# Prefix log-sum-exp along the sequence: a fourth load up front and an early store of part of the first tile on ScalarE's DMA ring

## Chip, cores and metric

One core of a Trainium2 chip, the other cores idle. The metric is the device time of one execution in microseconds (us); the profile's span, from the first to the last instruction, is some 1.8 us shorter. The runs of one kernel agree within 0.2%.

Three words are used throughout. A *ring* is the queue of transfers that one engine issues (SyncE's and ScalarE's here). A *run* is a stretch of consecutive bytes; the trace records each run as one packet. A transfer *lands* when the trace shows it complete, which releases those that wait for it.

## The reference

```python
# x: (4, 4096, 4128) float32
out[:, 0, :] = x[:, 0, :]
for t in range(1, S):
    mx = np.maximum(out[:, t - 1, :], x[:, t, :])
    out[:, t, :] = mx + np.log(np.exp(out[:, t - 1, :] - mx) + np.exp(x[:, t, :] - mx))
```

So out[t] is the logarithm of the running sum of exp(x), per column. The arrays are 270.5 MB each; every byte is read once and written once.

## The kernel before

A tile (a `Step`) holds 128 partitions x `r` consecutive rows x 4128 columns in float32; `r` is 3, or 2 for the first tile of the first sequence and the last tile of the others. It is worked on in place, in four chunks of 1024 columns (the last with 32 more, the tail). For each chunk ScalarE writes exp(x) as 16-bit numbers into the front half of the chunk's own columns, TensorE sums them into PSUM with triangular weights, and ScalarE writes the logarithm, row by row, over the same columns in 32 bits. When all chunks are done SyncE stores the tile.

```python
def load(self):
    full = xpool.tile([P, R, D], FP32, name="xt")      # 4 buffers
    self.xt = full[:, :self.r, :]
    self.half = self.xt.bitcast(FP16)                  # a 16-bit view of the same bytes
    nc.sync.dma_start(out=self.xt, in_=self.dram(x))

def store(self):
    nc.sync.dma_start(out=self.dram(out), in_=self.xt)

# Chunk
def exp(self):
    c0, w = self.c * CH, self.w
    nc.scalar.activation(
        self.t.half[:, :, 2 * c0:2 * c0 + w], self.t.xt[:, :, c0:c0 + w], ACT.Exp,
    )

def stage(self, j):
    t, c, pt = self.t, self.c, self.pt
    nc.scalar.activation(t.xt[:, j, c * CH:(c + 1) * CH], pt, ACT.Ln)
    # ... the next row's sum, or the carry to the next tile

# the order of issue
ahead = bufs - 1
for s in steps[:ahead]:
    s.load()
# ...
for g in range(len(chunks) + R - 1):
    for d in range(R - 1, -1, -1):
        if 0 <= g - d < len(chunks) and d < chunks[g - d].t.r:
            k = chunks[g - d]
            k.stage(d)
            if k.c == last and d + 1 == k.t.r:
                k.t.store()
                if stored + ahead < len(steps):
                    steps[stored + ahead].load()
                stored += 1
    if g + 2 < len(chunks):
        chunks[g + 2].exp()
    if g + 1 < len(chunks):
        chunks[g + 1].head()
```

Waits are not in the source: the tile framework works them out from which instruction reads and writes which part of a tile.

The softmax here doesn't subtract the row's maximum and nothing guards it: scores larger than these inputs give would overflow.

## Time and profile before

| | before |
|---|---|
| time, median of 4 runs | 1262.91 us |
| bytes over DMA | 541.07 MB |
| DMA engines (16), share of the span on SyncE's queue | 99.4% |
| rate at full DMA share | 432 to 436 GB/s |
| ScalarE busy | 75% |

The lines behind this table are in the prediction. One is the start of ScalarE's work, in the timeline (start, length in us, engine, line, operation, out<-in, count, and in brackets the idle time before it and what ended it). Before:

```profile
19.79 2.00 ACT L162 ACTIVATE xt<-pt 128x1024 f32<-128x1024 f32 x2
21.69 1.96 ACT L128 ACTIVATE xt<-xt 128x2112 f16<-128x2112 f32 x1
23.68 1.95 ACT L162 ACTIVATE xt<-pt 128x1024 f32<-128x1024 f32 x2
27.68 2.76 ACT L128 ACTIVATE xt<-xt 128x3072 f16<-128x3072 f32 x1 [2.06 <-DMA xt<-in_x_dram]
```

The first line is two logarithms, the second of chunk 0 and the first of chunk 1; the next is the exponential of chunk 3 (2 x 1056 = 2112 columns).

### The profile page before, as it was taken

What the parts mean: (1) busy time and instruction counts of PE and PEld (TensorE: products, weight loads), DVE (VectorE), ACT (ScalarE), POOL (GpSimd) and SP (SyncE); (2) the same over time, 40 slices, a digit from 0 to 9 for tenths busy, and PEclk for the clock granted to TensorE, in tenths of its full rate; (3) what the DMA queues carried; (4) which work ended last, traced back from release to release, by engine and by line L of the source; (5) the groups of instructions that cost most, each with busy time, mean ns of one, the idle gap of its engine ahead of it and who ended that gap; (6) DMA issues with size and microseconds to landing.
All of it is one profiled execution on the core that took longest, in us unless ns stands there. A gap on an engine that the chain in (4) does not pass through costs nothing.

```text
span 1261.0 us, 6165 instructions
## 1 busy us (share of the span) xinstructions
PE 688.7 (55%) x2268; PEld 237.0 (19%) x2268; DVE 451.4 (36%) x445; ACT 947.3 (75%) x733; POOL 2.2 (0%) x13
## 2 busy tenths in 40 slices
PE   3665554555555555655346555555634755664552
PEld 1222111111121111211112211111211211221120
DVE  2443333333333333334424333333442433333344
ACT  5997777777777777778569777777966977777794
POOL 0000000000000000000000000000000000000000
PEclk9887777777677777777768777787777777778786
DMA  9999999999999999999999999999999999999998
GB/s 411 410 439 431 432 427 434 438 430 432 433 437 431 432 432 436 432 427 436 431 433 436 437 429 431 436 436 432 430 434 435 432 431 432 434 435 431 433 422 347
DMA packets 12702, 541.46 MB, mean 429 GB/s; under 512 B 1408, under 2 KB 1408, under 8 KB 1408
## 3 DMA queue, kind: packets, MB, share of 16 engines
q1 hardware_dynamic: 12672, 541.07, 99.4%
q8 instruction: 18, 0.29, 0.1%
q14 instruction: 12, 0.10, 0.0%
HBM read 270.53 MB, written 270.53 MB: 429 GB/s over the span
## 4 chain that ended last, share of the span: by engine, by line
DMA 69%; ACT 21%; PE 5%; issue 2%; DVE 1%; SPq 0%; ACTq 0%
DMA xt<-in_x_dram 67%; ACT xt L128 11%; ACT xt L162 10%; PE pt L88 5%; DMA out_dram<-xt 2%; ACT xt L167 0%; SPq L116 0%; DVE carry L92 0%; DVE carry L93 0%; ACTq L231 0%; SPq L113 0%; ACTq L128 0%; PE qt L88 0%
## 5 line engine op out<-in xcount | busy, mean ns | idle before, releaser
L128 ACT ACTIVATE xt<-xt 128x3072 f16<-128x3072 f32 (+3 forms) x176 | 478.5, 2719 | 247.9 <-DMA xt<-in_x_dram 247.8
L88 PE MATMUL pt<-xt,ident 128*128 128x512 f16 x672 | 251.3, 470 | 530.7 <-ACT xt L162 530.4
L162 ACT ACTIVATE xt<-pt 128x1024 f32<-128x1024 f32 x512 | 487.6, 1030 | 2.5 <-PE pt L88 0.7
L92 DVE CAST carry<-pt 32x1024 f16<-32x1024 f32 x176 | 216.4, 1230 | 761.0 <-ACT xt L162 760.7
L88 PE MATMUL pt<-xt,excl 128*128 128x512 f16 x672 | 247.0, 504 | 0.0
L93 DVE TENSOR_TENSOR carry<-pt,carry 32x1024 f16<-32x1024 f32 x176 | 215.9, 1227 | 6.1
L88 PEld LDWEIGHTS <-ident 128*128 128x128 f16 x672 | 70.1, 104 | 677.7 <-issue 654.0
L88 PE MATMUL pt<-xt,incl 128*128 128x512 f16 x352 | 152.0, 526 | 23.6 <-ACT xt L128 15.0
L88 PEld LDWEIGHTS <-excl 128*128 128x128 f16 x756 | 92.5, 124 | 141.0 <-issue 108.1
L88 PE MATMUL pt<-carry,pick 128*128 128x512 f16 x320 | 109.8, 429 | 0.0
L88 PEld LDWEIGHTS <-incl 128*128 128x128 f16 x480 | 45.2, 111 | 129.7 <-DVE carry L93 95.2
L88 PEld LDWEIGHTS <-pick 128*128 128x128 f16 x360 | 40.6, 113 | 57.0 <-issue 34.3
L167 ACT ACTIVATE xt<-qt 128x96 f32<-128x96 f32 (+1 forms) x44 | 10.9, 249 | 45.7 <-PE pt L88 45.7
L92 DVE CAST carry_t<-qt 32x32 f16<-32x32 f32 x44 | 8.7, 197 | 25.5 <-ACT xt L167 25.4
L88 PE MATMUL qt<-xt,incl 128*128 128x64 f16 (+2 forms) x128 | 12.3, 196 | 0.0
L88 PE MATMUL qt<-xt,excl 128*128 128x64 f16 (+1 forms) x84 | 10.6, 187 | 0.0
L93 DVE TENSOR_TENSOR carry_t<-qt,carry_t 32x32 f16<-32x32 f32 x44 | 8.5, 193 | 1.5
L88 PE MATMUL qt<-carry_t,pick 128*128 128x96 f16 (+1 forms) x40 | 8.2, 204 | 0.0
L83 DVE MEMSET carry<- 128x512 uint32 x4 | 1.9, 485 | 1.1 <-PEq L220 1.0
L70 ACT ACT_TABLE_LOAD x1 | 1.3, 1283 | 0.8 <-PEq L220 0.8
L35 POOL TENSOR_SCALAR_AFFINE_SELECT pick<-pick 128x128 f16<-128x128 f16 x2 | 0.6, 294 | 0.1
L25 POOL TENSOR_SCALAR_AFFINE_SELECT incl<-incl 128x128 f16<-128x128 f16 x1 | 0.3, 294 | 0.0
(11 smaller groups left out, 1.9 us busy)
## 6 DMA issues: line engine op xcount, KB each, us to landing
xt<-in_x_dram SPq DMA_DIRECT2D x40, 6192.0 KB, 42.2
out_dram<-xt SPq DMA_DIRECT2D x40, 6192.0 KB, 28.1
xt<-in_x_dram SPq DMA_DIRECT2D x4, 4128.0 KB, 37.3
out_dram<-xt SPq DMA_DIRECT2D x4, 4128.0 KB, 23.0
```

What stands on the lines that cost most here:

```text
L25: nc.gpsimd.affine_select(out=t, in_=t, pattern=[[1, P]], compare_op=mybir.AluOpType.is_ge, fill=0.0, base=base, channel_multiplier=-1,)
L35: nc.gpsimd.affine_select(out=t, in_=t, pattern=[[step, P]], compare_op=mybir.AluOpType.not_equal, fill=1.0, base=base, channel_multiplier=1,)
L70: nc.scalar.preload_act_table_set("natural_log_exp_and_others")
L83: nc.vector.memset(t, 0.0)
L88: nc.tensor.matmul(pt, lhsT=w, rhs=rhs, start=start, stop=stop, skip_group_check=True)
L92: nc.vector.tensor_copy(cr[HI:HI + 32, :], pt[HI:HI + 32])
L93: nc.vector.tensor_tensor(out=cr[LO:LO + 32, :], in0=pt[HI:HI + 32], in1=cr[HI:HI + 32, :], op=mybir.AluOpType.subtract,)
L128: nc.scalar.activation(self.t.half[:, :, 2 * c0:2 * c0 + w], self.t.xt[:, :, c0:c0 + w], ACT.Exp,)
L162: nc.scalar.activation(t.xt[:, j, c * CH:(c + 1) * CH], pt, ACT.Ln)
L167: nc.scalar.activation(t.xt[:, :, t0:D], self.qt, ACT.Ln)
```

## The change

The intent, as far as the code shows it: keep loads in the queue past the first store, and take whatever a first store costs early, on another ring, while loads go on. Four loads are issued up front instead of three, and as soon as chunk 0 of the first tile is finished, its 1024 columns (2 rows of 4096 bytes in each partition, 1.05 MB) are stored by ScalarE's ring. The tile's later store on SyncE's ring leaves these columns out.

```diff
         def store(self):
-            nc.sync.dma_start(out=self.dram(out), in_=self.xt)
+            a = self.apart
+            nc.sync.dma_start(out=self.dram(out)[:, :, a:], in_=self.xt[:, :, a:])
+
+        def store_apart(self):
+
+            a = self.apart = CH
+            nc.scalar.dma_start(out=self.dram(out)[:, :, :a], in_=self.xt[:, :, :a])
...
-    for s in steps[:ahead]:
+    for s in steps[:bufs]:
         s.load()
...
                 k.stage(d)
+                if k is chunks[0] and d + 1 == k.t.r:
+                    k.t.store_apart()
                 if k.c == last and d + 1 == k.t.r:
                     k.t.store()
-                    if stored + ahead < len(steps):
+                    if bufs <= stored + ahead < len(steps):
                         steps[stored + ahead].load()
```

(`apart` is 0 for every other tile.)

More of the change, by code (lines that the diff above doesn't have):

```diff
@@ L103, in __init__ @@
             self.first = row == 0
+            self.apart = 0
         def dram(self, t):
```

## The prediction

> **What bounds the kernel now.** I began with the page: the table of busy time, then the row of DMA shares in the 40 slices, then the queues.
>
> ```profile
> PE 688.7 (55%) x2268; PEld 237.0 (19%) x2268; DVE 451.4 (36%) x445; ACT 947.3 (75%) x733; POOL 2.2 (0%) x13
> ...
> DMA  9999999999999999999999999999999999999998
> ...
> q1 hardware_dynamic: 12672, 541.07, 99.4%
> ```
>
> No compute engine is above 75%. The 16 DMA engines are at nine tenths or more in 39 of 40 slices, and the one queue that SyncE feeds takes 99.4% of their time. The kernel moves 541.07 MB whatever it does, and the change leaves every byte in. So the time is (bytes over rate) + (what the DMA engines lose), and a gain can only come out of the second term. I therefore cut the span at the landings of the first tiles and at the tail, and read the DMA share and the rate of each stretch.
>
> ```profile
> core 0: us, PE busy (x) PEld busy (x) DVE busy (x) ACT busy (x) POOL busy (x), PEclk, DMA share, GB/s
> 0.00:12.10 12.10, 0.00 (x0) 0.00 (x0) 1.97 (x5) 1.28 (x1) 2.17 (x13) 1.00 0.86 349
> 12.10:26.70 14.60, 8.33 (x19) 2.76 (x20) 4.39 (x4) 12.44 (x9) 0.00 (x0) 1.00 1.00 434
> 26.70:39.50 12.80, 7.37 (x25) 2.79 (x24) 5.83 (x7) 10.91 (x8) 0.00 (x0) 0.87 1.00 433
> 39.50:42.40 2.90, 1.35 (x6) 0.43 (x5) 0.00 (x0) 2.87 (x4) 0.00 (x0) 1.00 1.01 273
> 42.40:52.10 9.70, 5.60 (x28) 2.31 (x28) 2.83 (x3) 9.67 (x8) 0.00 (x0) 1.00 1.01 436
> 52.10:66.70 14.60, 9.53 (x32) 3.21 (x32) 7.38 (x8) 13.92 (x12) 0.00 (x0) 0.88 1.00 432
> 66.70:600.00 533.30, 303.47 (x997) 103.92 (x996) 189.18 (x186) 408.86 (x316) 0.00 (x0) 0.76 1.00 433
> 600.00:1200.00 600.00, 325.60 (x1070) 112.10 (x1070) 211.79 (x207) 448.05 (x347) 0.00 (x0) 0.76 1.00 433
> 1200.00:1226.00 26.00, 17.25 (x58) 5.88 (x57) 12.43 (x12) 22.95 (x19) 0.00 (x0) 0.81 1.01 435
> 1226.00:1234.30 8.30, 5.48 (x17) 1.88 (x17) 3.62 (x6) 8.19 (x8) 0.00 (x0) 0.79 0.42 181
> 1234.30:1261.00 26.70, 4.69 (x23) 1.74 (x21) 12.02 (x12) 8.11 (x9) 0.00 (x0) 0.69 0.92 396
> ```
>
> The last two columns matter. At share 1.00 the rate is 433 to 436 GB/s for pure loads (12.1 to 39.5), for the first store (42.4 to 52.1) and for the mix, so the mix of directions is worth nothing. There are four losses: the start (12.1 us at share 0.86, 1.7 us), **a stall at 39.5 to 42.4**, where the engines are occupied but move only 273 GB/s, the gap near the end (8.3 us at 0.42, 4.8 us) and the ending (26.7 us at 0.92, 2.1 us). In the stall each of the 16 engines is on its last packet of the third load, just before the first store; in the records of single packets these 16 packets average 2.9 us where such a packet of 49,536 bytes has a median of 1.829 us. The loss is 2.9 - 1.83 = 1.1 us. No later turn from load to store shows one.
>
> The list of DMA issues on SyncE gives the order:
>
> ```profile
> 0.80 1.33 SPq L113 DMA_DIRECT2D xt<-in_x_dram  x3
> 37.00 0.35 SPq L116 DMA_DIRECT2D out_dram<-xt  x1
> 37.39 0.44 SPq L113 DMA_DIRECT2D xt<-in_x_dram  x1
> 63.44 0.34 SPq L116 DMA_DIRECT2D out_dram<-xt  x1
> 63.88 0.38 SPq L113 DMA_DIRECT2D xt<-in_x_dram  x1
> ```
>
> So the ring never ran dry: the first store was there at 37.0, 2.5 us before the stall and 4.4 us before the third load would have ended.
>
> **What the Trainium skill says.** "DMA: Bandwidth & Descriptors", section "Where 436 GB/s comes from", states a fabric ceiling of 435.2 GB/s for the 16 ports; the 433 to 436 above agree, so there is no headroom in the rate. The same page, "Issuing engines are not separate DMA queues", says that DMAs started by different engines run on the same 16 DMA engines and interleave; so the second ring adds no bandwidth, and this trace, with one issuing engine, neither shows nor contradicts it. Its section "Queues, rings and completion order" says that a DMA engine takes turns between rings packet by packet; what a packet is here the trace leaves open, but an instruction fetch on another queue (16,384 bytes at 58.09 us) is seen served between two packets of one load. I found no page that states a cost of the first store.
>
> **The change, part by part.**
>
> *Fourth load up front.* Its issue moves from 37.39 us to about 2. Before, it stood in the ring behind the first store; now that store stands behind it. The same five transfers fill the ring to the same moment. Worth by itself: 0, except that other traffic follows the third load.
>
> *The early piece.* Tile 0 has 2 rows per partition, so 2 x 128 runs of 4,096 bytes (1.05 MB) go on ScalarE's ring after the second logarithm of chunk 0. In the timeline two logarithms start at 19.79, 1.0 us each, chunk 0's first, so this issue comes at about 20.9. It costs ScalarE some 0.35 us (SyncE's issue takes 0.34 to 0.44), inside slack: ScalarE stands idle for 2.06 us before 27.68, waiting for the second load. If the rings take turns at every run, a 4 KB run follows each load packet, and the piece needs 16 turns of about 2 us to drain; the second load, which ends at 26.75, is later by about three runs, 0.5 us. If all 16 runs on an engine go at once, by up to 16 x 0.16 = 2.5 us.
>
> *Shorter runs.* Packets of 49,536 and 33,024 bytes take 1829 and 1222 ns: 36.8 ns per 1,000 bytes and 8 ns fixed. The first store had 8 runs on each engine and now has 16 + 16, so 24 x 8 ns = +0.2 us.
>
> *The stall.* This must be the aim: to take the first-store cost while another ring has loads to serve. If so, -1.1 us. If the engine itself stands still, 0.
>
> *The buffer.* The fifth load now waits for the whole first store, which ends at about 66 us rather than 53, so it is issued at some 68 rather than 63.88. Meanwhile the second store, issued at 63.4 to 64, holds the ring from 66 until 81. It is hidden: 0.
>
> *The end.* After the fifth load the sequence is unchanged, and the gap at 1226 to 1234 follows the last load's landing: the page's chain has that load landing at 1220.7, then ScalarE's 13 us to the store before last. It moves with what came before and neither grows nor shrinks: 0.
>
> Sum, stall hidden: 1262.97 - 1.1 + 0.2 = 1262.1 us. Stall kept: 1263.2 us.
>
> **The rivals.** *One: the stall moves to 21 us.* For it: it looks like a once-only cost of the first store, and it held up a load's packet, not a packet of the store, so it reached across transfers; a load beside it on another ring may be held in the same way. The first loads are slow too (first packets 0.6 us over on average). Against it: the two stood in one ring. This makes 1263.2.
>
> *Two: the second store comes late.* The ring's first five transfers, stall gone, end at about 12.2 + 3 x 14.65 + 2.5 + 7.4 = 66.1 us. The second store is issued at 63.44 plus the delay of the second load, and an issue takes about 1 us to its first packet (0.80 to 1.82 at the start). With 0.5 us of delay it is ready at 64.9, in time. With 2.5 us it comes at 66.9 and 0.8 us is lost, which gives back most of the gain: 1262.9. If the old stall came from a store issued only a few us before the ring ran out, the second store, with less lead than the first had, would meet it again: 1263.2 or more.
>
> *Three: a large gain,* if pure loads with later stores ran faster. The windows speak against it: 434 for loads, 436 for the store.
>
> **Range and chances.** I give the hidden stall about 0.5, the moved stall 0.35, a late second store or some other loss 0.1, and a little more gain than reckoned 0.05. Weighted, that is near 1262.5. The three timed runs before differ by 0.31 us, so noise is small beside the theories; I take 1261.4 to 1263.7. Two per cent is 25 us, and all losses together are below 10 us: faster 0.01, same 0.98, slower 0.01.
>
> **What would show it right or wrong.** Right: DMA share 1.00 at 433 or so through 39.5 to 42.4, with no stretch at 270 near 21 to 24; the second store issued within 0.6 us of 63.4; the fifth load issued about 4 us later than before; the gap near the end as long as before but some 1 us earlier. A stretch of low rate at 21 to 24 would show rival one; a share under 1 or a slow stretch near 66, rival two. The prediction is wrong if the gap near the end changes its length, if the early piece slows the loads by more than its bytes, or if the time moves by over 2 us either way: then something of the steady state depends on the start that I have not seen.

## The result, and the profile after

| | before | after |
|---|---|---|
| time, median of 4 runs | 1262.91 us | 1293.96 us |
| range | 1262.83 to 1263.14 | 1293.83 to 1294.14 |
| span of the profiled run | 1261.0 us | 1292.4 us |

The ratio is 1.0246, with a 95% interval of 1.0228 to 1.0263: slower by 31 us. All ratios here are the mean time of one kernel's fast runs over that of the other's in the same rounds, so not quite the ratio of the medians. The prediction was 1262.5 us, with "slower" at 0.01.

Where did the 31 us go? First the page, the busy tenths of the DMA engines and their rate in 40 slices of 32 us:

```profile
DMA  9729999999999999999999999999999999999998
GB/s 409 343 123 393 437 430 429 437 431 430 437 430 431 437 431 427 440 429 430 435 429 438 431 435 433 431 433 432 433 434 432 433 431 434 431 437 428 436 425 349
```

Only the second, third and fourth slice are low. Cut more finely, the columns are as in the prediction (DMA share and GB/s last; a packet is counted whole in the stretch in which it begins, so a short stretch can show more than 1.00, or too little):

```profile
55.40:58.60 3.20, 0.00 (x0) 0.00 (x0) 0.00 (x0) 2.83 (x2) 0.00 (x0) 1.00 0.64 279
59.20:70.20 11.00, 6.78 (x20) 2.45 (x20) 6.02 (x7) 9.90 (x9) 0.00 (x0) 1.00 0.00 0
70.20:78.00 7.80, 6.55 (x22) 2.47 (x21) 1.32 (x2) 7.44 (x5) 0.00 (x0) 0.78 0.96 408
78.00:96.70 18.70, 12.12 (x42) 4.18 (x42) 8.55 (x9) 18.02 (x16) 0.00 (x0) 0.82 0.00 1
...
1257.40:1265.70 8.30, 5.43 (x16) 1.88 (x17) 3.67 (x5) 8.30 (x9) 0.00 (x0) 0.79 0.45 193
```

The DMA engines stand still for 11.0 us and again for 18.7 us, 29.7 us in all, with some tenths more at the edges. (The 0.64 of the first line comes from that way of counting: by the records of single packets the engines are busy until 58.5 to 59.1 us.) The gap near the end is the same 8.3 us at 0.45 (0.42 before), so nothing else of size changed. SyncE's issues show why the engines had nothing to do:

```profile
0.80 1.95 SPq L114 DMA_DIRECT2D xt<-in_x_dram  x4
69.06 27.20 SPq L118 DMA_DIRECT2D out_dram<-xt  x2
96.36 0.37 SPq L114 DMA_DIRECT2D xt<-in_x_dram  x1
```

The four loads are done by 59 us. The first store is issued at 69.06 (before: 37.00), the second at the end of the merged line, about 95.9 (before: 63.44), both 32 us late. What held the first store is in ScalarE's timeline:

```profile
19.85 1.02 ACT L169 ACTIVATE xt<-pt 128x1024 f32<-128x1024 f32 x1
20.91 0.64 ACTq L123 DMA_DIRECT2D out_dram<-xt  x1
21.59 1.02 ACT L169 ACTIVATE xt<-pt 128x1024 f32<-128x1024 f32 x1 [0.72 <-ACT xt L169]
55.73 1.96 ACT L135 ACTIVATE xt<-xt 128x2112 f16<-128x2112 f32 x1 [33.12 <-DMA out_dram<-xt]
```

The exponential of chunk 3 of the first tile, which followed without a pause before, now waits 33.1 us, and what ends the wait is the landing of the early piece. All of ScalarE's later work comes after it: the first exponential of the second tile, whose load had ended by 28 us, starts at 59.55. The list of DMA issues says how long the piece took:

```profile
out_dram<-xt ACTq DMA_DIRECT2D x1, 1024.0 KB, 34.8
```

34.8 us for 1.05 MB. In the records of single packets this ring serves one run of 4,096 bytes (159 ns) after each load packet of 49,536 bytes (1829 ns) on each DMA engine: 16 runs, one per 1.98 us (two at 27 and at 43 us, where a load ends), from 25 to 27 us on. The last run ends at 53.6 us; on most engines one more load packet goes by before the record that marks the end, at 55.4.

**Is the wait needed?** No byte is shared. The piece reads columns 0 to 1023 of both rows; the exponential of chunk 3 writes into the front half of columns 3072 and up. But the built program has the wait. This is ScalarE's instruction in the listing of the built program, before and after:

```
before  Activation xt<-xt 128x2x1056 [waits Activation]
after   Activation xt<-xt 128x2x1056 [waits DMAHW2]
```

(The name behind "waits" is that of a counter: ScalarE's own before, and after the one that the piece's DMA raises.)

The first logarithm of chunk 1, issued right after the piece (21.59 us), writes row 0 of columns 1024 to 2047, which also lies between the piece's first and last address, and has no such wait. It writes through the 32-bit view, like the piece; the exponential writes through the 16-bit view. So I supposed that **views of different types are compared from first to last address, without the gap between the rows**. Row 0 and row 1 of the piece are 4128 columns apart, and that span covers the rest of row 0. Two builds, not run, agree: a 32-bit write to both rows of chunk 3, put in before the exponential, gets no wait for the piece, while the exponential after it does; and with the piece read through the 16-bit view, the 32-bit logarithm of chunk 1 gets the wait.

### The profile page after: what moved, and what is told of

Its sections match the earlier page's. It is cut to its first block, busy times and chain, and to the rows that moved or that the text cites. A ratio compares the mean times of both kernels' runs of the same rounds, so it can differ in the third digit from the quotient of the medians.

```text
span 1292.4 us, 6166 instructions
## 1 busy us (share of the span) xinstructions
PE 689.4 (53%) x2268; PEld 237.3 (18%) x2268; DVE 451.4 (35%) x445; ACT 947.4 (73%) x733; POOL 2.2 (0%) x13
## 3 DMA queue, kind: packets, MB, share of 16 engines
q10 hardware_dynamic: 272, 1.05, 0.2%
## 4 chain that ended last, share of the span: by engine, by line
DMA 69%; ACT 21%; PE 5%; issue 2%; DVE 1%; SPq 0%; ACTq 0%
DMA xt<-in_x_dram 65%; ACT xt L135 11%; ACT xt L169 9%; PE pt L88 5%; DMA out_dram<-xt 4%; DVE carry L92 0%; DVE carry L93 0%; ACT xt L174 0%; SPq L118 0%; ACTq L240 0%; ACTq L135 0%; SPq L114 0%; PE qt L88 0%
## 6 DMA issues: line engine op xcount, KB each, us to landing
out_dram<-xt ACTq DMA_DIRECT2D x1, 1024.0 KB, 34.8
```

## The experiments

Theory A: the whole loss is this wait for the landing. Rival B: the first store behind the fourth load delays the buffer and starves the DMA engines. Rival C: the second ring (its turns, or its issue on ScalarE) costs the time. The first four ran on one chip and shared runs of the kernel before (1262.83 us median of 7), the other four on one chip with another 7 (1262.92 us).

### e1_loads_only: one part alone, the four loads

```diff
-                if k is chunks[0] and d + 1 == k.t.r:
-                    k.t.store_apart()
```

> Four loads up front, no early piece; nothing waits for a piece. Theory A (the whole loss is the wait of the exponential of chunk 3 of the first tile for the early piece to land, 33.1 us in the trace after): 1262 to 1263.7 us, no wait of ScalarE on an output store, DMA share 1.00 from 12 to 1226 us. Rival B (putting the first store behind the fourth load delays the fifth load, and the DMA engines run out of work): most of the 31 us stays, 1285 us or more, with an idle stretch between 59 and 97 us.

Measured: 1262.73 us, ratio 0.9999 [0.9984, 1.0014]. ScalarE waits for no store in the first 60 us; all that it waits for a DMA is:

```profile
ACT xt L135 <- DMA xt<-in_x_dram: 13.2, 2, 11.1
```

(us in total, times, longest.) The fifth load was issued at 68.94 us instead of 63.88 and it cost nothing. Rival B is out.

### e3_split_rows: the whole change without the wait

```diff
-            nc.scalar.dma_start(out=self.dram(out)[:, :, :a], in_=self.xt[:, :, :a])
+            for j in range(self.r):
+                nc.scalar.dma_start(out=self.dram(out)[:, j, :a], in_=self.xt[:, j, :a])
...
-            nc.scalar.activation(
-                self.t.half[:, :, 2 * c0:2 * c0 + w], self.t.xt[:, :, c0:c0 + w], ACT.Exp,
-            )
+            rows = range(self.t.r) if self.t is steps[0] and self.c == last else [slice(None)]
+            for j in rows:
+                nc.scalar.activation(
+                    self.t.half[:, j, 2 * c0:2 * c0 + w], self.t.xt[:, j, c0:c0 + w], ACT.Exp,
+                )
```

With a piece for each row and an exponential for each row, no span from first to last address touches another. Two builds that were not run show that both edits are needed: with the exponential split (and the tail's logarithm), but the piece whole, its row 0 still waits; with the piece split alone, the exponential waits for the piece of row 1.

> The whole change, but the early piece is issued row by row (two DMAs) and the exponential of chunk 3 of the first tile as two instructions of one row each; the built program then holds no wait of ScalarE for a piece. Same bytes, same ring, same four loads. Theory A: 1262 to 1263.7 us, the piece still takes over 30 us to land, nobody waits for it. Rival C (the interleaving of the two rings, or the issue on ScalarE, costs the time): about 1294 us as after the change.

Measured: 1263.22 us, ratio 1.0003 [0.9988, 1.0018]. The pieces land as slowly, and nobody minds (the line has the median of the two: 20.0 us for row 0 and 34.7 us for row 1, against 34.8 us for the whole piece in the change):

```profile
out_dram<-xt ACTq DMA_DIRECT2D x2, 512.0 KB, 27.3
```

The same bytes on the same ring beside the same loads, and the 31 us are gone. Rival C is out.

### e4_row0 and e4_row1: the same bytes, at two addresses

```diff
-            nc.scalar.dma_start(out=self.dram(out)[:, :, :a], in_=self.xt[:, :, :a])
+            nc.scalar.dma_start(out=self.dram(out)[:, 0, :a], in_=self.xt[:, 0, :a])   # e4_row1: 1
```

(SyncE's store of the first tile is two DMAs then, one for the rest of this row and one for the other row.)

> The early piece is row 0 of chunk 0 only (128 runs of 4096 bytes). Its span of addresses ends before chunk 3's columns, and the built program has no wait for it. Theory A with 'the dependency is worked out from first to last address, without the gap between the rows': 1262 to 1263.7 us. Rival C: loses about half of the 31 us.

> The early piece is row 1 of chunk 0 only: as many bytes and runs as in e4_row0, but its addresses lie between the first and last address that the exponential of chunk 3 writes, and the built program has the wait. Theory A: 8 turns of 1.98 us on each DMA engine instead of 16, so the piece lands at about 41 to 42 us instead of 55.7, the ScalarE wait is some 19 us, and the time is 1263 + (41.5 - 25.5) + 0.5 = about 1279.5 us, where 25.5 us is the landing at which the second store would come just in time. If the wait is no part of it: as e4_row0.

Measured: row 0, 1263.19 us, ratio 1.0002 [0.9986, 1.0019]; row 1, 1278.66 us, ratio 1.0126 [1.0111, 1.0141]. Row 1's trace has the wait:

```profile
ACT xt L139 <- DMA out_dram<-xt: 19.0, 1, 19.0
```

Both pieces are 0.5 MB in 128 runs and land after 19.9 and 20.4 us. Row 0's piece needs only the first logarithm of chunk 0 and is issued 1.2 us earlier (19.87 against 21.03 us); besides that, the only difference that the builds show on ScalarE before the first store is the wait. This also fits what I supposed of the comparison of views: row 0's span ends before chunk 3's columns begin, row 1's lies inside the exponential's span. It is shown for these builds; the framework's own code was not read.

### e2_piece_only, e5_half_cols, e6_sync_ring: move the landing

```diff
# e2_piece_only: three loads up front, as before
-    for s in steps[:bufs]:
+    for s in steps[:ahead]:
...
-                    if bufs <= stored + ahead < len(steps):
+                    if stored + ahead < len(steps):
# e5_half_cols
-            a = self.apart = CH
+            a = self.apart = CH // 2
# e6_sync_ring
-            nc.scalar.dma_start(out=self.dram(out)[:, :, :a], in_=self.xt[:, :, :a])
+            nc.sync.dma_start(out=self.dram(out)[:, :, :a], in_=self.xt[:, :, :a])
```

> The early piece on ScalarE's ring, with the wait for it, but only three loads up front. Theory A, with the piece taking one run per turn as long as loads are in the other ring: the loads end at about 43 us, then the rest of the piece (6 or 7 runs per DMA engine, 0.16 us each) drains at once, it lands at about 45.5 us instead of 55.7; the DMA engines stand still from about 44.6 to 60 and some 4 us more before the second store, 20 us in all: about 1283 us. If the fourth load had no part in it: 1294 us; if it took both parts of the change together to lose time: 1263 us.

> The whole change with a piece of half the columns: the same 256 runs, 2048 bytes each. If the landing goes by turns (one run of the piece per 1.83 us load packet on each DMA engine): 16 turns of 1.91 us, landing at about 54.5 us, time about 1292.5 us, 1 us or so below the changed kernel. If it goes by bytes: landing near 38 us and time near 1276 us.

> The whole change with the piece issued by SyncE, in the same ring as the loads. If the wait for the landing is the cause whatever the ring: the piece stands behind four loads, lands at about 59.7 us, the time is 1263 + (59.7 - 25.5) + 0.5 = about 1298 us, slower than with ScalarE's ring. If the second ring is the culprit: about 1263 us.

Measured: 1283.53 us (1.0164), 1292.76 us (1.0237) and 1299.08 us (1.0286). All kernels with the wait, in order of the time at which it let ScalarE go on:

| kernel | exponential of chunk 3 starts at, us | wait, us | time, us | over before, us |
|---|---|---|---|---|
| e4_row1 | 41.5 | 19.0 | 1278.66 | 15.8 |
| e2_piece_only | 45.4 | 22.9 | 1283.53 | 20.6 |
| e5_half_cols | 54.3 | 31.7 | 1292.76 | 29.8 |
| the change | 55.7 | 33.1 | 1293.96 | 31.1 |
| e6_sync_ring | 60.5 | 38.7 | 1299.08 | 36.2 |

The last column is the second less 24.3 to 25.7 us in all five rows: microsecond for microsecond, the time follows the landing. The start and the wait are those of the profiled run, the time is the median; with the profiled runs' own times the difference is 24.2 to 24.7 us; e4_row1's runs spread most, 1277.82 to 1279.77 us, and its profiled run was the slowest. (In the change, the second store's first packet comes 41 us after the landing, and the ring would have had work until about 66.5 us, hence some 25 us of grace.) What matters is the landing and not the ring as such: SyncE's own ring, where the piece stands behind all four loads, is the worst. Half the bytes in as many runs helped by 1.4 us only:

```profile
out_dram<-xt ACTq DMA_DIRECT2D x1, 512.0 KB, 33.4
```

So on a ring beside long loads the landing is counted in runs, not in bytes. With fewer loads in the other ring (e2) the rest of the piece drained once the loads had ended.

### The stall at the first turn from load to store

The prediction hoped to hide the 1.1 us that the DMA engines lost at 39.5 to 42.4 us. It is still there in e1, on the last packets of the fourth load, before the first store:

```profile
53.90:57.30 3.40, 2.45 (x10) 0.86 (x10) 0.99 (x3) 2.81 (x3) 0.00 (x0) 1.00 1.01 301
```

301 GB/s at share 1.01 for 3.4 us: (1 - 301 / (1.01 x 433)) x 3.4 = 1.1 us. It is there in e3 too, where the early pieces had been written from 23 us on and had landed by 55.6 us:

```profile
56.90:59.20 2.30, 0.12 (x1) 0.00 (x0) 0.30 (x1) 2.30 (x3) 0.00 (x0) 1.00 1.05 302
```

So it is not the cost of the first bytes stored, which the pieces would have paid; in both kernels it comes where the loads on SyncE's ring end and a store follows. That it belongs to that ring is not shown: in e2 the last packets of the third load, at 41 us, took 2.4 us instead of 1.83 on average, and nothing stood behind them on SyncE's ring, only the rest of the piece on ScalarE's. In the change, packets are slow at two turns: at 109.6 us (2.5 us on average), from the second store to the fifth load, and at 125 us (2.8 us), from there to the third store. Why the later turns show little of it is open. In the kernel before, the 16 DMA engines end a transfer within 0.8 us of each other up to 53 us and 3 to 4 us apart from 97 us on, so they no longer turn together; but that is an observation, not a test.

### e8_short_end: another loss, tried and missed

No version of the change beat the kernel before, so I tried the one idle stretch of size that is left, at its end.

```diff
         if b == 0:
             parts.reverse()
+        if b == B - 1:
+            parts[-2:] = [2, 2, 1]
```

(And the tail's logarithm and carry are moved out of the branch for further rows, so that a tile with one row has them too.)

> The kernel before with another end: the last sequence's last two tiles of 3 and 2 rows per partition become 2, 2 and 1. It aims at the only idle DMA time of size, 4.8 us between 1226 and 1234 us, where the store before last waits for three exponentials and seven logarithms after the last load has landed. With one row in the last tile that work is about 6.5 us against a store in the ring of 9.8 us that began 2 us before the landing. Expected 1258.5 to 1260.5 us; if the gap is not set by that work, 1263 us.

Measured: 1263.40 us, ratio 1.0003 [0.9988, 1.0018]: a miss. The gap did shrink, but the very end got longer. First this kernel, then the kernel before, each with the gap and the ending:

```profile
1237.70:1243.00 5.30, 4.10 (x10) 1.28 (x9) 3.78 (x5) 4.20 (x7) 0.00 (x0) 0.50 0.62 268
...
1257.00:1261.60 4.60, 0.00 (x0) 0.00 (x0) 0.00 (x0) 0.00 (x0) 0.00 (x0) 0.50 0.13 54
```

```profile
1258.00:1261.00 3.00, 0.00 (x0) 0.00 (x0) 0.00 (x0) 0.00 (x0) 0.00 (x0) 0.50 0.03 11
```

By these shares the gap costs 5.3 x 0.38 = 2.0 us instead of 4.8; by the packet records, with each packet's own end, the DMA engines are idle for 2.3 us there instead of 4.1. By the same records most DMA engines were done at 1257.7 us, 1.3 us earlier than before (1259.0), but a single one worked until 1260.1 (before: 1259.7). It looks as if the gap had let the latest engine catch up, so that the mean loss over 16 engines was never all to be had: the last engine sets the end. That was not tested further.

## Why the prediction was wrong

**The step that failed** is in the early piece: "It costs ScalarE some 0.35 us [...] inside slack". The issue took 0.64 us, a trifle. What the prediction left out is that a store reads the tile, and that a later instruction that writes the tile may have to wait until the store has landed. It asked this for SyncE alone, under "The buffer" (the fifth load waits for the first tile's buffer), and not for ScalarE, which goes on writing this same tile in place. The term that was missing from the sum is this wait of 33.1 us. It made the first two stores 32 us late each; the DMA engines had loads until 59 us and then stood still for 29.7 us, with 0.7 us more at the edges of these stretches. The rest of the 31 us is one more slow turn than before, from the second store to the fifth load:

```profile
109.50:112.00 2.50, 1.87 (x8) 0.76 (x9) 0.39 (x2) 2.50 (x2) 0.00 (x0) 1.00 1.13 357
```

That is (1 - 357 / (1.13 x 433)) x 2.5 = 0.7 us. e3 and the pair e4 show that the loss goes when the wait goes.

It could have been seen blind. The order of instructions had not changed beyond one added issue, and I looked at no more than that with care; the waits in the same listing show the added one. The prediction even worked out the slow landing ("16 turns of about 2 us") and asked only what it does to the loads.

**What held.** The kernel is bound by DMA at a fixed rate, and nothing is to be had there (432 to 436 GB/s before; 433 in the change from 127.7 to 1257.4 us). The fourth load is worth nothing by itself (e1). The issue came at 20.91 us as reckoned and the piece needed 16 turns, one run at a time. The fifth load was hidden (e1: issued at 68.94 us against "some 68"). The gap near the end kept its length, so the prediction's own reading of a time over 2 us off, that "something of the steady state depends on the start", does not apply: the loss is over by 128 us.

**What else failed.** "If so, -1.1 us" for the stall, at a chance of 0.5: it was not hidden in any kernel. Rival one had it move "to 21 us" with the early store. No slow packet was seen there: in e1 and e3 it came at the end of the fourth load instead. Rival two came nearest: the second store was late, but by 32 us and through ScalarE's wait, not by 0.8 us through a late second load. "24 x 8 ns = +0.2 us" for shorter runs can't be told from noise: e3 is 0.4 us above the kernel before, within its interval. The reading of the gap near the end was off too: 4.8 us comes from a share that counts packets where they begin, and the packet records give 4.1. And the chance of 0.01 for "slower" came from adding up the losses that were in the old profile, which says nothing about a wait that is new.

## What to carry to other kernels

Before storing part of a tile early, ask who still writes that tile, and read the waits of the built program, not only its order: a store is a reader, and a framework may see an overlap where no byte is shared, above all between views of different types or across rows with gaps. What such a wait costs is set by when the DMA lands, and a small transfer of short runs beside queued transfers of long runs lands late: count its runs, not its bytes. In a DMA-bound kernel a wait on a compute engine is free only as long as the queue has work for its whole length.

## What the Trainium skill lacked or had wrong

- "DMA: Bandwidth & Descriptors", section "Queues, rings and completion order", says that a DMA engine drains a packet of typically 9 to 17 descriptors from one ring before it switches. In the packet records here the switch came after every run: one run of 4,096 bytes, then one of 49,536, 16 turns of 1.98 us; halving the run to 2,048 bytes left the landing at 33.4 us against 34.8.
- The same page, section "Issuing engines are not separate DMA queues", says that DMAs of different issuing engines interleave; it lacks what follows for a ring of short runs beside one of long runs: 1.05 MB took 34.8 us, where 16 runs of 0.16 us alone would, by estimate, be 2.5 us.
- Its section "Rules for kernel authors" advises to issue a DMA early and to wait for it late. It lacks that the late wait may not be the author's to place: no page that I read says that a store of one part of a tile may hold up writes to another part of it. Here that was a wait of 33.1 us, with no byte in common.
- No page that I read has the loss where loads end and a store follows: 1.1 us in the kernel before and in the kernel with four loads alone.
